# Low halves of streamed weights by an adding DMA in place of a subtraction on VectorE

## The chip, the cores and the metric

The kernel runs on one core of a Trainium2 chip. A core has five engines with queues of their own: TensorE (PE, matmuls), VectorE (DVE), ScalarE (ACT), GpSimd (POOL) and SyncE (SP), which issues most loads. Sixteen DMA engines move the data; transfers are issued from SP's queue or from GpSimd's. The metric is the device time of one execution in microseconds, the median of several runs.

## The reference

A trunk of two layers over 1024 tokens of width 1024, batch 1, fp32, with a vector `c` that modulates both layers:

```python
def even_mixer(h, ...):                       # layer 0
    xa, ga, q, k, v, gb = split(h @ w_in)
    ya = rg_lru(conv4(xa), ...) * silu(ga)
    yb = stick_breaking_attention(rms(q), rms(k), v) * silu(gb)   # 8 heads of 128
    return concat([ya, yb]) @ w_out
def odd_mixer(h, ...):                        # layer 1
    u, g = split(h @ w_in)
    y = gelu(s5_ssm(u, ...))                  # 64 groups of 16 channels, 64 states each
    y = y * sigmoid(y @ glu_w + glu_b)
    return (y * silu(g)) @ w_out
# each layer: x = x + gate * mixer(rms_norm(x) * g * (1 + scale) + shift),
# shift, scale, gate from silu(c) @ ada_w + ada_b
```

## The kernel before

Every fp32 matrix that enters a projection is split into two rounded halves, hi = round(w) and lo = round(w - hi), and a product is the sum of three: hi by hi, hi by lo, lo by hi. Activations lie transposed in SBUF as 8 tiles of 128 x 1024, with a hi and a lo tile each. A weight block is a tile of 128 x 1024 (512 KB) and feeds one projection: 48 matmuls of 512 columns, six for each of 8 k-tiles (lines 120 to 125 of `proj_k`); the fifth of the six is the first that reads the block's low half. In attention, q, k and v of a head come from three blocks of `wqkv` side by side in one pair of tiles, `wqkv_hi` and `wqkv_lo`, and matmuls of 384 columns (lines 771 to 773).

The blocks are streamed. `w_fetch` loads the next of `w_order` one ahead of use: 0 to 7 are the gate weights of the attention heads, 8 to 19 those of the LRU stage, 20 to 35 the output projection of layer 0 (`woe`), 36 to 51 the input projection of layer 1 (`wod`, u and g blocks), 52 to 59 the GLU. There are two hi, two lo and two raw buffers; a hi and a lo buffer come free when the projection before the last has read them. `load_split` issues the load on SP's queue, ScalarE rounds the high half (`w_hi`, line 72), VectorE subtracts (`w_lo`, line 75). `load_qkv` does the same for the three blocks of the next head while the present head still runs. The first three blocks of layer 1 (`w_shifted`) are also read raw by VectorE for the shift's share.

The stages follow one another: norm and head 0; attention head by head, with gates and the next head's q, k, v as filling work, the adaLN columns (`ada_raw`, which share the raw buffers) and the S5 preparation on VectorE; the LRU stage; the output projection, eight blocks against `ya`, eight against `yb`, meanwhile VectorE makes rotation tables which GpSimd stores (`rot_s`); layer 1, where projections alternate with S5 matmuls; eight GLU blocks; the last projection, whose factors GpSimd computes (`st_w`). Only TensorE's order is the order of the code. On the other engines the scheduler of the framework places instructions by its own estimate of when they can run, so an edit moves neighbours as well. Each engine executes its queue in order.

In attention the weights of one query block come from `keep` and `beta`: ScalarE writes both from the scores (lines 820, 823), VectorE scans `keep` (826) and multiplies `beta` by it (827), and TensorE transposes `beta` (837).

Of the kernel before, what the change touches and what calls it, by code (L numbers as in the profile page):

```python
# [9 lines left out]
F32 = mybir.dt.float32  # L10
# [3 lines left out]
AF = mybir.ActivationFunctionType  # L14
ALU = mybir.AluOpType
PSUM = bass.MemoryType.PSUM

P = 128
# [36 lines left out]
class Trunk:  # L55
# [21 lines left out]
    def load_split(self, src, hi, lo):  # L77
# [2 lines left out]
        self.split(raw, hi, lo)  # L80
        return raw

    def w_next(self, ahead=1):

        self.w_fetch(self.w_used + 1 + ahead)
        self.w_used += 1
        return self.w_ready.pop(0)
# [13 lines left out]
    def w_fetch(self, n):  # L101

        while self.w_loaded < min(len(self.w_order), n):
            hi = self.wp.tile([P, 1024], F32R, name="w_hi", tag="whi", bufs=2)
            lo = self.wp.tile([P, 1024], F32R, name="w_lo", tag="wlo", bufs=2)
            raw = self.load_split(self.w_order[self.w_loaded], hi, lo)
            if self.w_loaded in self.w_shifted:
                self.shifted(raw)
            self.w_ready.append((hi, lo))
            self.w_loaded += 1  # L110

# [112 lines left out]
    def run(self):  # L224
        nc, I = self.nc, self.I
        self.cp = self.pool("const")
        self.rp = self.pool("raw", bufs=2)
        self.wp = self.pool("w")
        psp = self.pool("psum", space=PSUM)
        self.bank = [psp.tile([P, 512], F32, name=f"bank{i}") for i in range(8)]  # L230
        self.pair_i = 0
        self.w_order = [I["wfm"][16 + h] for h in range(8)] + [I["wfm"][8]]
        self.lru_order = [(x[:2], int(x[2:])) for x in LRU_ORDER.split()]
        names = {"ga": "ga", "xa": "xa", "ga": "ga", "cv": "conv", "gt": "gates", "dc": "decays"}
        self.lru_order = [(names[kind], m) for kind, m in self.lru_order]
        self.w_order += [I["wfm"][m + (8 if kind == "ga" else 0)] for kind, m in self.lru_order if kind in ("ga", "xa")]
        for half in range(2):
            self.w_order += [I["woe"][m][:, half * 1024:(half + 1) * 1024] for m in range(8)]
        self.s5_order = self.plan_s5()
        self.w_odd, self.w_shifted, self.wsh = len(self.w_order), set(), []  # L240
        self.w_order += [I["wod"][m + (8 if kind == "g" else 0)] for kind, m in self.s5_order if kind in "ug"]
        self.w_order += [I["wglu"][m] for m in range(8)]
        self.w_used = self.w_loaded = 0
        self.w_ready = []
        self.setup()
        self.hp = self.pool("h0")
        self.hh = self.hp.tile([P, KT, T], F32R, name="h_hi")
        self.hl = self.hp.tile([P, KT, T], F32R, name="h_lo")
        self.layer0_norm()
        self.attention()  # L250
        self.lru()
        self.out_even()
        self.layer1()
        psp.release()
# [61 lines left out]

    def load_qkv(self, hd, c):
        cs = slice(c * 1024, (c + 1) * 1024)
        self.load_split(self.I["wqkv"][hd][:, cs], self.wqh[:, cs], self.wql[:, cs])

    def layer0_norm(self):

# [1316 lines left out]
```

## Time and profile before

| | us |
|---|---|
| median of 3 runs | 1342.17 |
| lowest, highest | 1341.04, 1342.34 |
| the profiled execution, its own time | 1343.34 |
| its span | 1341.3 |
| TensorE busy | 1316.6 |
| VectorE busy | 1010.6 |
| ScalarE busy | 651.8 |
| GpSimd busy | 228.9 |

The span is what the hardware profiler saw from the first instruction to the last; 2.0 us lie around it. A group of instructions has a line number of the kernel, the tile written and the tiles read, the busy time and the mean of one, and the idle time in front of it with what ended it. A line can be that of a helper: line 75 is every subtraction of a split, so the tile's name tells which. A wait that several events end is put down to the last of them.

### The profile page before, as it was taken

What the parts mean: (1) busy time and instruction counts of PE and PEld (TensorE: products, weight loads), DVE (VectorE), ACT (ScalarE), POOL (GpSimd) and SP (SyncE); (2) the same over time, 40 slices, a digit from 0 to 9 for tenths busy, and PEclk for the clock granted to TensorE, in tenths of its full rate; (3) what the DMA queues carried; (4) which work ended last, traced back from release to release, by engine and by line L of the source; (5) the groups of instructions that cost most, each with busy time, mean ns of one, the idle gap of its engine ahead of it and who ended that gap; (6) DMA issues with size and microseconds to landing.
All of it is one profiled execution on the core that took longest, in us unless ns stands there. A gap on an engine that the chain in (4) does not pass through costs nothing.

```text
span 1341.3 us, 18939 instructions
## 1 busy us (share of the span) xinstructions
PE 1316.6 (98%) x7020; PEld 1137.7 (85%) x7020; DVE 1010.6 (75%) x1826; ACT 651.8 (49%) x1218; POOL 228.9 (17%) x411
## 2 busy tenths in 40 slices
PE   7998999999999999999999999999999999999998
PEld 3898989898999999988878878888888888888777
DVE  7949977777787868787999787866588669755653
ACT  6545454545454545455998621132463434632421
POOL 1012322222222222210000000000000000000784
PEclk9999999999999999999999999999999999999999
DMA  8443141414141414213112164342458778444331
GB/s 324 166 149 95 58 142 37 146 34 145 34 145 34 147 33 158 85 63 110 36 40 67 61 230 136 115 145 99 135 164 247 229 246 245 122 163 133 108 112 76
DMA packets 73356, 168.22 MB, mean 125 GB/s; under 512 B 9552, under 2 KB 35408, under 8 KB 73264
## 3 DMA queue, kind: packets, MB, share of 16 engines
q1 hardware_dynamic: 62256, 128.40, 31.3%
q0 software_dynamic: 11008, 38.62, 7.8%
q8 instruction: 55, 0.90, 0.3%
q14 instruction: 37, 0.30, 0.1%
HBM read 126.16 MB, written 40.83 MB: 125 GB/s over the span
## 4 chain that ended last, share of the span: by engine, by line
PE 78%; DVE 13%; ACT 3%; issue 3%; DMA 2%; POOL 1%; DVEq 0%; ACTq 0%; POOLq 0%
PE bank L120 6%; PE bank L121 6%; PE bank L123 6%; PE bank L122 6%; PE bank L124 6%; PE bank L125 6%; PE bank L771 6%; PE bank L773 6%; PE bank L772 6%; PE bank L837 2%; PE bank L199 2%; PE bank L197 2%; PE bank L198 2%; DMA ada_raw<-ada 2%; PE bank L849 1%
## 5 line engine op out<-in xcount | busy, mean ns | idle before, releaser
L771 PE MATMUL bank<-wqkv_hi,h_hi 128*128 128x384 f32 x512 | 173.6, 339 | 0.0
L773 PE MATMUL bank<-wqkv_hi,h_lo 128*128 128x384 f32 x512 | 172.3, 337 | 0.0
L772 PE MATMUL bank<-wqkv_lo,h_hi 128*128 128x384 f32 x512 | 172.3, 337 | 0.0
L72 ACT CAST w_hi<-w_raw 128x1024 fp32r<-128x1024 f32 x60 | 63.0, 1050 | 193.5 <-PE bank L123 148.5
L75 DVE TENSOR_TENSOR w_lo<-w_raw,w_hi 128x1024 fp32r<-128x1024 f32 x60 | 73.0, 1218 | 41.2 <-ACT w_hi L72 41.1
L771 PEld LDWEIGHTS bank<-wqkv_hi,h_hi 128*128 128x128 f32 x512 | 96.6, 189 | 0.3
L772 PEld LDWEIGHTS bank<-wqkv_lo,h_hi 128*128 128x128 f32 x512 | 96.6, 189 | 0.4
L773 PEld LDWEIGHTS bank<-wqkv_hi,h_lo 128*128 128x128 f32 x512 | 96.5, 189 | 0.0
L120 PE MATMUL bank<-h_hi,w_hi 128*128 128x512 f32 x224 | 89.1, 398 | 0.0
L122 PE MATMUL bank<-h_hi,w_hi 128*128 128x512 f32 x224 | 87.6, 391 | 0.8 <-DVE xc L1014 0.8
L124 PE MATMUL bank<-h_hi,w_lo 128*128 128x512 f32 x224 | 87.7, 392 | 0.4 <-DVE w_lo L75 0.4
L121 PE MATMUL bank<-h_lo,w_hi 128*128 128x512 f32 x224 | 87.7, 391 | 0.0
L123 PE MATMUL bank<-h_lo,w_hi 128*128 128x512 f32 x224 | 87.5, 390 | 0.0
L125 PE MATMUL bank<-h_hi,w_lo 128*128 128x512 f32 x224 | 87.4, 390 | 0.0
L778 ACT ACTIVATE nat<-bank 128x128 f32<-128x128 f32 x64 | 17.7, 277 | 141.3 <-PE bank L773 137.9
L826 DVE TENSOR_TENSOR_SCAN keep<-keep,diag 128x1024 f32<-128x1024 f32 (+3 forms) x64 | 86.2, 1347 | 0.1
L314 POOL TENSOR_SCALAR ss<-ss 128x2 f32<-128x2 f32 x64 | 28.6, 446 | 296.6 <-ACT nat L779 296.1
L820 ACT ACTIVATE keep<-bank,ss 128x512 f32<-128x512 f32 (+2 forms) x96 | 54.5, 597 | 21.7 <-PE bank L819 20.1
L783 DVE SCALAR_TENSOR_TENSOR nat<-bank,ss,gqk 128x128 f32<-128x128 f32 x64 | 22.1, 345 | 47.9 <-PE bank L837 25.9
L823 ACT ACTIVATE beta<-bank,ss 128x512 f32<-128x512 f32 (+3 forms) x96 | 54.4, 600 | 0.0
L290 DVE SCALAR_TENSOR_TENSOR ada_raw<-ada_raw,cs 128x1024 f32<-128x1024 f32 x39 | 47.6, 1220 | 7.8 <-DMA ada_raw<-ada 7.5
L315 POOL TENSOR_TENSOR ss<-ss,mh 128x2 f32<-128x2 f32 x64 | 51.9, 810 | 5.3
(436 smaller groups left out, 3739.2 us busy)
## 6 DMA issues: line engine op xcount, KB each, us to landing
ada_raw<-ada SPq DMA_DIRECT2D x39, 512.0 KB, 3.9
w_raw<-wqkv SPq DMA_DIRECT2D x21, 512.0 KB, 3.6
w_raw<-wfm SPq DMA_DIRECT2D x20, 512.0 KB, 3.6
w_raw<-woe SPq DMA_DIRECT2D x16, 512.0 KB, 3.8
w_raw<-wod SPq DMA_DIRECT2D x16, 512.0 KB, 4.4
x<-xT SPq DMA_DIRECT2D x8, 512.0 KB, 7.1
cx_s<-ce POOLq DMA_DIRECT2D x16, 256.0 KB, 2.7
win_s<-wsb POOLq DMA_DIRECT2D x16, 256.0 KB, 3.5
```

Of the source, the lines that this page charges most:

```text
L72: nc.scalar.copy(hi, raw)
L75: nc.vector.tensor_sub(lo, raw, hi.bitcast(F32))
L120: nc.tensor.matmul(ps[0], wh[:, k, :], rh[k][:, h0], start=first, stop=False)
L121: nc.tensor.matmul(ps[0], wh[:, k, :], rl[k][:, h0], start=False, stop=False)
L122: nc.tensor.matmul(ps[1], wh[:, k, :], rh[k][:, h1], start=first, stop=False)
L123: nc.tensor.matmul(ps[1], wh[:, k, :], rl[k][:, h1], start=False, stop=False)
L124: nc.tensor.matmul(ps[0], wl[:, k, :], rh[k][:, h0], start=False, stop=last)
L125: nc.tensor.matmul(ps[1], wl[:, k, :], rh[k][:, h1], start=False, stop=last)
L771: nc.tensor.matmul(ps[:, 0:384], hh[:, k, ts], wqh[:, ks], start=(k == 0), stop=False)
L772: nc.tensor.matmul(ps[:, 0:384], hh[:, k, ts], wql[:, ks], start=False, stop=False)
L773: nc.tensor.matmul(ps[:, 0:384], hl[:, k, ts], wqh[:, ks], start=False, stop=(k == KT - 1))
L826: v.tensor_tensor_scan(rev, rev, self.diag[:, T - n:T][:, ::-1], 0.0, op0=ALU.mult, op1=ALU.max)
```

## The change

A new `load_split_dma` takes the place of `load_split` for 68 blocks: the blocks 0 to 9 and 20 to 59 of `w_order` except the three shifted ones (47), and the 21 of `load_qkv`. It loads the raw tile as before and lets ScalarE round the high half; then ScalarE writes the negated high half into the low tile, -round(w) from the raw tile, and a DMA issued by GpSimd adds the block once more from DRAM onto that tile, which leaves w - hi. The subtraction on VectorE is gone for these blocks. The ten LRU blocks 10 to 19, the shifted ones, head 0's first q, k, v blocks and all splits of activations stay.

```diff
--- before.py
+++ after.py
@@ -80,6 +80,15 @@
         self.split(raw, hi, lo)
         return raw
 
+    def load_split_dma(self, src, hi, lo):
+
+        nc = self.nc
+        raw = self.rp.tile([P, 1024], F32, name="w_raw", tag="raw")
+        nc.sync.dma_start(raw, src)
+        nc.scalar.copy(hi, raw)
+        nc.scalar.activation(lo, raw, AF.Copy, scale=-1.0)
+        nc.gpsimd.dma_start(lo, src, accum_op=ALU.add)
+
     def w_next(self, ahead=1):
 
         self.w_fetch(self.w_used + 1 + ahead)
@@ -103,9 +112,12 @@
         while self.w_loaded < min(len(self.w_order), n):
             hi = self.wp.tile([P, 1024], F32R, name="w_hi", tag="whi", bufs=2)
             lo = self.wp.tile([P, 1024], F32R, name="w_lo", tag="wlo", bufs=2)
-            raw = self.load_split(self.w_order[self.w_loaded], hi, lo)
-            if self.w_loaded in self.w_shifted:
-                self.shifted(raw)
+            if self.w_loaded in self.w_plain:
+                self.load_split(self.w_order[self.w_loaded], hi, lo)
+            elif self.w_loaded in self.w_shifted:
+                self.shifted(self.load_split(self.w_order[self.w_loaded], hi, lo))
+            else:
+                self.load_split_dma(self.w_order[self.w_loaded], hi, lo)
             self.w_ready.append((hi, lo))
             self.w_loaded += 1
 
@@ -234,6 +246,7 @@
         names = {"ga": "ga", "xa": "xa", "ga": "ga", "cv": "conv", "gt": "gates", "dc": "decays"}
         self.lru_order = [(names[kind], m) for kind, m in self.lru_order]
         self.w_order += [I["wfm"][m + (8 if kind == "ga" else 0)] for kind, m in self.lru_order if kind in ("ga", "xa")]
+        self.w_plain = range(10, len(self.w_order))
         for half in range(2):
             self.w_order += [I["woe"][m][:, half * 1024:(half + 1) * 1024] for m in range(8)]
         self.s5_order = self.plan_s5()
@@ -316,7 +329,7 @@
 
     def load_qkv(self, hd, c):
         cs = slice(c * 1024, (c + 1) * 1024)
-        self.load_split(self.I["wqkv"][hd][:, cs], self.wqh[:, cs], self.wql[:, cs])
+        self.load_split_dma(self.I["wqkv"][hd][:, cs], self.wqh[:, cs], self.wql[:, cs])
 
     def layer0_norm(self):
```

The lines of the changed kernel stand 13 further down from `w_fetch` on. Three places show what else moves.

VectorE, head 0 of attention. Between the scan (`keep<-keep,diag`) and the product `beta<-beta,keep` of the first query block there stood before one adaLN pass (`ada_raw`) and six products of the S5 preparation (`t`, `bb`):

```order
L826 SCALAR_TENSOR_TENSOR keep<-keep,diag 128x1024
L633 TENSOR_TENSOR s5small<-s5small 128x32
L290 SCALAR_TENSOR_TENSOR ada_raw,mod<-ada_raw,cs 128x1024
L641 TENSOR_TENSOR t_1104<-bb,s5small 128x512
L642 TENSOR_TENSOR t_1105<-bb,s5small 128x512
L643 TENSOR_TENSOR bb<-bb,s5small 128x512
L645 TENSOR_TENSOR bb<-bb,s5small 128x512
L644 TENSOR_TENSOR bb<-bb,t_1105 128x512
L646 TENSOR_TENSOR bb<-bb,t_1104 128x512
L1130 TENSOR_SCALAR lsmall<-cols 128x8
L827 TENSOR_TENSOR beta<-beta,keep 128x1023
```

and now, from the last three of those products on:

```order
L657 TENSOR_TENSOR bb<-bb,t_1107 128x512
L658 TENSOR_TENSOR bb<-bb,s5small 128x512
L701 TENSOR_TENSOR ce<-craw,pw 128x2x144
L659 TENSOR_TENSOR bb<-bb,t_1106 128x512
L1143 TENSOR_SCALAR lsmall<-cols 128x8
L839 SCALAR_TENSOR_TENSOR keep<-keep,diag 128x1024
L1144 TENSOR_TENSOR lsmall<-lsmall,cols 128x8
L690 COPY bd<-bb 64x8x16
L222 TENSOR_SCALAR lsmall<-lsmall 128x8
L840 TENSOR_TENSOR beta<-beta,keep 128x1023
```

The products stand ahead of the scan and the adaLN pass has gone elsewhere; three small operations are left between scan and product.

GpSimd, from attention into the output stage, before (`yb_s` is the last head's result on its way to DRAM, `rot_s` the rotation tables):

```order
L727 DMA win_s_1119<-wsb 128x512
L734 DMA rp_s_1135<-rpad 128x240
L967 DMA yb_s_616<-yb 128x1024
L1220 DMA rot_s_7771<-rot 128x1024
L1220 DMA rot_s_7772<-rot 128x1024
L1220 DMA rot_s_7773<-rot 128x1024
```

and now:

```order
L740 DMA win_s_1121<-wsb 128x512
L747 DMA rp_s_1137<-rpad 128x240
L980 DMA yb_s_618<-yb 128x1024
L90 DMA w_lo<-woe 128x1024 x2
L1233 DMA rot_s_7811<-rot 128x1024
L90 DMA w_lo<-woe 128x1024 x2
L1233 DMA rot_s_7812<-rot 128x1024
```

The low halves of two blocks go ahead of the first `rot_s`, the third waits behind it.

ScalarE, first half of layer 1 (`x<-x,mod,gain` is the modulation of the normed activations, `h_hi` their split, `ub` and `ut` the early u blocks), before:

```order
L1253 COPY ub<-bank_75 128x1
L1260 ACTIVATE x_7271<-x_7271,mod,gain 128x1024
L1298 ACTIVATE ut<-ut,ub 128x512 x2
L72 CAST w_hi<-w_raw 128x1024
L1260 ACTIVATE x_7271<-x_7271,mod,gain 128x1024 x4
L72 CAST h_hi<-x_7271 128x1024 x3
L1253 COPY ub<-bank_76 128x1
L72 CAST h_hi<-x_7271 128x1024 x2
```

and now:

```order
L1266 COPY ub<-bank_75 128x1
L1273 ACTIVATE x_7303<-x_7303,mod,gain 128x1024
L1311 ACTIVATE ut<-ut,ub 128x512 x2
L88 CAST w_hi<-w_raw 128x1024
L1273 ACTIVATE x_7303<-x_7303,mod,gain 128x1024 x4
L89 ACTIVATE w_lo<-w_raw 128x1024
L72 CAST h_hi<-x_7303 128x1024 x2
L1266 COPY ub<-bank_76 128x1
L72 CAST h_hi<-x_7303 128x1024 x2
```

The pass that writes the negated half (`w_lo`) stands behind four modulations and ahead of the splits.

## Rows read from the trace of the kernel before

**Rows 1.** Page: busy time by engine; a group: busy us, mean ns, idle before

```profile
PE 1316.6 (98%) x7020; PEld 1137.7 (85%) x7020; DVE 1010.6 (75%) x1826; ACT 651.8 (49%) x1218; POOL 228.9 (17%) x411
...
L72 ACT CAST w_hi<-w_raw 128x1024 fp32r<-128x1024 f32 x60 | 63.0, 1050 | 193.5 <-PE bank L123 148.5
```

**Rows 2.** VectorE by line, splits of streamed weights: busy us, mean ns

```profile
L75 DVE TENSOR_TENSOR w_lo<-w_raw,w_hi 128x1024 fp32r<-128x1024 f32 x60 | 73.0, 1218 | 41.2 <-ACT w_hi L72 41.1
...
L75 DVE TENSOR_TENSOR wqkv_lo<-w_raw,wqkv_hi 128x1024 fp32r<-128x1024 f32 x21 | 25.7, 1222 | 7.0 <-ACT wqkv_hi L72 7.0
```

**Rows 3.** Waits of TensorE, whole span: us in total, times, longest

```profile
PE bank L837 <- DVE beta L827: 3.1, 4, 2.1
...
PE bank L121 <- DVE rot L1205: 0.6, 1, 0.6
```

**Rows 4.** Timeline of TensorE in head 0: start, duration, idle before, releaser

```profile
114.03 0.66 PE L798 MATMUL bank<-ident,nat 128*128 128x128 f32 x4 [1.59 <-DVE nat L783]
...
131.74 1.09 PE L837 MATMUL bank<-ident,beta 128*128 128x128 f32 x8 [2.07 <-DVE beta L827]
```

**Rows 5.** Windows in head 0: us, busy by engine, clock, DMA share, GB/s

```profile
113.00:114.00 1.00, 0.00 (x0) 0.00 (x0) 1.00 (x3) 0.00 (x0) 0.75 (x1) 1.00 0.65 90
132.00:137.00 5.00, 5.00 (x24) 5.00 (x23) 4.55 (x11) 3.47 (x8) 2.87 (x4) 0.66 0.00 0
```

**Rows 6.** Timeline of VectorE in head 0

```profile
112.50 1.21 DVE L75 TENSOR_TENSOR wqkv_lo<-w_raw,wqkv_hi 128x1024 fp32r<-128x1024 f32 x1
113.64 0.34 DVE L783 SCALAR_TENSOR_TENSOR nat<-bank,ss,gqk 128x128 f32<-128x128 f32 x1
...
123.35 2.28 DVE L826 TENSOR_TENSOR_SCAN keep<-keep,diag 128x1024 f32<-128x1024 f32 x1
...
130.46 1.22 DVE L827 TENSOR_TENSOR beta<-beta,keep 128x1023 f32<-128x1023 f32 x1
```

**Rows 7.** Timeline of ScalarE in head 0

```profile
122.67 0.70 ACT L823 ACTIVATE beta<-bank,ss 128x511 f32<-128x511 f32 x1
```

**Rows 8.** DMA issues: queue, count, KB each, median us to landing

```profile
w_raw<-woe SPq DMA_DIRECT2D x16, 512.0 KB, 3.8
...
rot_s<-rot POOLq DMA_DIRECT2D x8, 512.0 KB, 2.9
...
us<-ut POOLq DMA_DIRECT2D x8, 512.0 KB, 7.2
...
gs_s<-sg POOLq DMA_DIRECT2D x8, 512.0 KB, 5.1
...
ada_w<-adak SPq DMA_DIRECT2D x2, 512.0 KB, 9.0
```

**Rows 9.** Timeline of GpSimd: output stage and end of layer 1

```profile
788.15 0.54 POOL L1220 DMA_DIRECT2D rot_s<-rot  x1 [163.00 <-DVE rot L1219]
...
1164.34 0.53 POOL L1311 DMA_DIRECT2D gs_s<-sg  x1 [12.39 <-DVE sg L537]
```

**Rows 10.** Window in the output stage, columns as in rows 5

```profile
775.00:780.00 5.00, 4.43 (x19) 3.30 (x19) 3.74 (x13) 2.00 (x2) 0.00 (x0) 1.00 1.02 419
```

**Rows 11.** Timeline of ScalarE: output stage and start of layer 1

```profile
762.27 1.05 ACT L72 CAST w_hi<-w_raw 128x1024 fp32r<-128x1024 f32 x1
...
783.40 1.06 ACT L72 CAST w_hi<-w_raw 128x1024 fp32r<-128x1024 f32 x1 [5.69 <-DMA w_raw<-woe]
...
973.11 4.64 ACT L1260 ACTIVATE x<-x,mod,gain 128x1024 f32<-128x1024 f32 x4
```

**Rows 12.** Timeline of TensorE: first read of a low half in four projections

```profile
768.41 0.39 PE L124 MATMUL bank<-ya,w_lo 128*128 128x512 f32 x1
...
791.23 0.39 PE L124 MATMUL bank<-ya,w_lo 128*128 128x512 f32 x1
...
981.52 0.39 PE L124 MATMUL bank<-h_hi,w_lo 128*128 128x512 f32 x1
...
1170.87 0.39 PE L124 MATMUL bank<-y_hi,w_lo 128*128 128x512 f32 x1
```

## The prediction

> **What bounds the kernel now.** I read the busy times first: TensorE works 98% of the span, VectorE 75%, ScalarE 49%, GpSimd 17% [rows 1]. So what the change takes from VectorE counts only where TensorE stands still, and I read TensorE's waits next. VectorE's share of them that the change can touch is small: four waits for `beta` (3.1 us, of which one is 2.07), one for `nat` (1.59), one of 0.6 (near 778) that the list puts on a memset, behind a low half of `ya` that VectorE had just split [rows 3, 4]. The other idle time lies at the start, inside the LRU stage, in the last phase where GpSimd subtracts, or on loads, and is left as it is. The clock comes third: after the 2.07 us the granted clock averages 0.66 over 132 to 137 us, with part of it at the lower level (1.2 of 2.4 GHz); while TensorE stood still for 1.59 us at 113 the row shows 1.00 [rows 4, 5]. The first stall therefore cost 2.07 + 5 x 0.34 = 3.8 us.
>
> **What goes and comes.** 68 loads change (47 of `w_fetch`, 21 of `load_qkv`). VectorE loses 47 x 1.218 + 21 x 1.222 = 82.9 us [rows 2]; ScalarE gains a second pass of the size of its first, 68 x 1.05 = 71 us [rows 1], which brings it to 54%; GpSimd gains 68 issues of about 0.54 us [rows 9], 37 us; the DMA engines move 68 x 0.524 = 35.7 MB more. None of these totals is a time: the terms are four places.
>
> **Gain, attention.** The order of VectorE in head 0 shows where 2.07 us go. Before, one pass over adaLN weights and six 512-wide products stand between the scan and `beta`; now the products come ahead of the scan, in the time of three removed subtractions (3.66 us), and the pass elsewhere. ScalarE has the scan's second half ready at 122.67 + 0.70 = 123.4 in either kernel; then the scan's 2.28 us and two or three small operations, so `beta` starts near 125.9 instead of 130.46 and TensorE asks at 129.67 [rows 4, 6, 7]. The stall goes, and the half-clock stretch with it: 3.8 us. The other three `beta` waits, 3.1 - 2.07 = 1.0, follow head boundaries where three subtractions leave VectorE; I take all of it. The `nat` wait: a subtraction ran from 112.50 until `nat` started at 113.64 [rows 6]. Two are gone from its front, but small operations of the S5 preparation have moved in there, and ScalarE's second pass delays the sums of squares by up to 1.05. Between 0 and 1.59 I take 0.4. The 0.6 near 778 goes, since two subtractions ahead of that split are gone. Gain: 3.8 + 1.0 + 0.4 + 0.6 = 5.8 us.
>
> GpSimd's queue now also holds the adding transfers ahead of norm operations at each head boundary, and they wait there for ScalarE's pass. I cost that at nothing: `nat` is waited for once in the whole trace, and TensorE has scores and gates of the old head to do meanwhile; without that cover it would be a pass of 1.05 us in each of seven heads.
>
> **The new chain.** Elsewhere a weight's low half was ready 1.2 us after its high half. Now it is high half, ScalarE's negative pass (1.05), GpSimd's issue, landing. Call L the time from issue to landing. The trace of before has no adding transfer. Below it is bounded by GpSimd's quickest 512 KB, 2.9 us, above by the slowest 512 KB load of the list, 9.0 [rows 8]. The same bytes of the output weights land in 3.8 by the plain queue; a second operand to be read makes it longer by up to 0.52 MB at the rate of the DMA engines when full, 419 GB/s, 1.25 us [rows 8, 10]. I take L = 5.0, nearest the 3.8 row.
>
> The Trainium skill (DMA: Bandwidth & Descriptors, "Anatomy of one DMA — SWDGE (gpsimd) path") fits a transfer issued by GpSimd as 2.0 us + bytes / 436e3, 3.2 us for 512 KB. It also says (Collectives: The Full Stack, "The bandwidth ceiling") that a DMA's add reads both operands, which would make the estimate 4.4; GpSimd's own rows of 2.9 to 7.2 us in this trace [rows 8] do not follow such a fit. By 4.4 the sum below would come out at -2.8, the edge of the faster case.
>
> **Where L is paid.** Both weight buffers are free only when the projection before the last is done, so there is one projection for all of it: the first low halves of the first and third output blocks are read 22.8 us apart, 0.6 of it waiting [rows 3, 12], 11.1 us for one. Four places have less.
> First projection of the output stage: ScalarE is behind with the end of the LRU, starts the high half at 762.27, negates until 764.4; the first low half is read at 768.41 [rows 11, 12]: TensorE waits L - 4.0.
> Third one: its raw tile lands late behind eight loads of `x`; high half at 783.40, negated by 785.5; but in GpSimd's queue the store of `rot_s` stands ahead, which started at 788.15 and comes at most 1.2 earlier (one subtraction less on VectorE), plus 0.54 to issue: 787.5 to 788.7. Read at 791.23 [rows 9, 11, 12]: L - 3.7 to L - 2.5, I take L - 3.1. It contains the first wait, since a delayed TensorE also asks later; it is not added to it. The second weight's transfer runs beside those loads at full DMA engines [rows 10] and has 7 us, so it is covered unless L passes 7.
> Fourth projection of layer 1, the first one after the three shifted weights: four modulations of 1.16 us are queued on ScalarE between the high half and the negative pass, until 977.7; negated at 978.8, read at 981.52 [rows 11, 12]: L - 2.7. Before, VectorE did this subtraction meanwhile and nothing waited.
> First GLU projection: its transfer stands on GpSimd behind the store of `gs_s`, which starts at 1164.34 and takes 0.53; the low half is read at 1170.87 [rows 9, 12]: L - 6.0.
> Everything else has more room: in attention and where S5 work lies between the projections an L of 9 is covered; the other output and GLU projections pay from L of about 9 on (11.1 us less two passes and an issue).
> The 35.7 MB may slow the loads that S5 work waits for, by a microsecond or two; I leave that out of the sum and in the range.
>
> **The sum.** At L = 5: third output projection 1.9, fourth of layer 1 2.3, nothing at the GLU. The clock: 1.59 us of idle time kept it, 2.07 did not [rows 4, 5], so the 2.3 gets 1.7 on top, the 1.9 none. Losses 5.9, gain 5.8: +0.1 on the profiled 1343.34 us (span 1341.3). That run lies 1.2 above the median of the three (1342.17), which the next kernel's will be compared with: 1343.44 - 1.17, forecast **1342.3 us**.
> For other L: 4.0 gives 0.9 + 1.3 - 5.8 = -3.6 (1338.6); 4.4, 1.3 + 1.7 - 5.8 = -2.8; 6.0, 2.9 + 3.3 + 3.4 (two clock losses) - 5.8 = +3.8 (1346.0); 7.0, 3.9 + 4.3 + 3.4 + 1.0 - 5.8 = +6.8 (1349.0); 9.0, 5.9 + 6.3 + 3.4 + 3.0 - 5.8 = +12.8 (1355.0), before any steady projection pays.
>
> **Rivals.**
> Faster: the adding transfer lands like GpSimd's quick stores (2.9 to 4.4) and only the attention gain is left: 1336.6 to 1339.4. For it speak the rows of 2.9 and an idle queue [rows 8, 9], against it the second operand.
> Slower: it lands in 5.3 to 7 us. Mechanism and place are the same two first reads of a low half; it decides from L = 5.3 on, because then both stalls pass 2.07 us and both cost the clock too: 1345 to 1349. For it speak GpSimd's stores of 5.1 and 7.2 us and the full DMA engines around 778 [rows 8, 10].
> Much slower: the addition itself is slow, 7 to 9 us or more. From 9 on each of some twenty back-to-back projections waits: 1349 to 1357 and beyond. No row speaks for it or against it.
> It changes nothing: VectorE's stalls only move to what is late next (ScalarE, with its 71 us more, in front of the same `beta`), and the transfers stay hidden: within 2 us of today. Against it: ScalarE idles half the time.
>
> **How the numbers follow.** Landing in 4.4 to 5.3 (gain and loss cancel) 0.35; faster 0.26; slower 0.23; much slower 0.13; nothing changes 0.03. 0.2% is 2.7 us, about what can be told apart here. Faster by more 0.26, within 0.38, slower 0.36. The range of 1337.5 to 1354 leaves out the lowest fifth of the faster case (0.05) and most of the much slower one (0.1).
>
> **What would show it.** The attention step holds if the wait for `beta` at about 130 us and the 0.66 after it are gone; it fails if TensorE still waits there for VectorE, or for ScalarE. The list of DMA issues will give L as `w_lo` from GpSimd; TensorE's waits must then name that transfer in the output stage near 790 and in layer 1 near 981, with L - 3.1 and L - 2.7. Waits in every projection from 800 on mean the much slower case. If L is 5 and neither place waits, the chain of release and queues is wrong, not the price; if `nat` waits at head boundaries, the cover that I gave GpSimd's queue was not there.

## The result: 6.5% slower, more than half of it in attention

The changed kernel takes 1429.31 us (median of 4 runs, 1426.79 to 1432.22) against 1341.61 us for the kernel before (4 runs beside it, 1341.03 to 1342.34). The ratio is 1.0654, 95% interval 1.0631 to 1.0677: slower by 88 us, far outside the range that was given (1337.5 to 1354).

The page of the kernel after, in the columns of [rows 1] (first line), then its queues (packets, MB, share of 16 engines' span):

```profile
PE 1340.0 (94%) x7020; PEld 1154.2 (81%) x7020; DVE 937.5 (66%) x1758; ACT 715.7 (50%) x1286; POOL 281.4 (20%) x479
...
q1 hardware_dynamic: 62256, 128.40, 29.6%
q0 software_dynamic: 20800, 74.27, 20.5%
```

The work moved as the diff says: VectorE lost 73 us against [rows 1], ScalarE gained 64, GpSimd 53. But TensorE, with the same 7020 matmuls, is busy 23.4 us longer, most of it by the clock (an estimate of 20 us, from windows of 0.25 us: eleven stretches at a lowered clock, where the kernel before has one), and idle for 1428.7 - 1340.0 = 88.7 us instead of 24.7. 23.4 + 64.0 is the whole difference of the spans, 87.4 us.

The list of DMA issues of the kernel after, columns as in [rows 8], then one row and the second queue of the kernel before:

```profile
ada_raw<-ada SPq DMA_DIRECT2D x39, 512.0 KB, 6.0
w_raw<-wqkv SPq DMA_DIRECT2D x21, 512.0 KB, 4.0
wqkv_lo<-wqkv POOLq DMA_DIRECT2D x21, 512.0 KB, 8.6
...
w_lo<-woe POOLq DMA_DIRECT2D x16, 512.0 KB, 7.8
...
w_lo<-wod POOLq DMA_DIRECT2D x13, 512.0 KB, 8.2
```
```profile
q0 software_dynamic: 11008, 38.62, 7.8%
...
ada_raw<-ada SPq DMA_DIRECT2D x39, 512.0 KB, 3.9
```

The adding transfer, L in the prediction, lands in 7.8 to 8.6 us (medians of its groups), not in 5.0. And a load that the diff doesn't touch became slower: `ada_raw`, 6.0 us where the same row of before has 3.9.

TensorE's waits in the kernel after, columns as in [rows 3]:

```profile
PE bank L850 <- DVE beta L840: 35.9, 6, 6.8
PE bank L136 <- DMA w_lo<-woe: 9.7, 4, 3.6
PE bank L1393 <- DMA tz<-rp_s: 8.0, 4, 2.7
...
PE bank L136 <- DMA w_lo<-wod: 4.7, 1, 4.7
PE bank L136 <- DMA w_lo<-wglu: 4.3, 3, 2.6
```

The first line is the surprise: the product whose wait was to vanish, 3.1 us before, is now waited for 35.9 us, at six head boundaries (in heads 1 to 6, where the first is head 0). It waits for VectorE, the engine that the change relieved.

Where the time came in, by the moment at which TensorE reaches the same instruction (timelines of four kernels, us; e1 and e2 are the halves of the change, below):

```
                                         before   after    e1       e2
first low half, output stage             768.41   821.57   818.52   770.09
first product, layer 1                   943.32  1007.56   993.47   950.97
first product of S5 input, layer 1       991.70  1062.96  1041.85  1007.06
first high half, GLU                    1169.94  1250.73  1219.11  1192.81
first low half, last phase              1257.48  1343.44  1306.67  1285.89
```

After minus before: 53.2 us up to the output stage (3.6 of them its first wait), 11.1 in the output stage, 16.5 in layer 1 (7.0 of them in its first four projections, before the S5 input), 5.2 in the GLU stage, 1.4 behind it.

### One head boundary

VectorE at the boundary of heads 0 and 1 (the expectations below call it that of heads 1 and 2), kernel before (start, duration, instruction, idle before): the adaLN passes (L290), the scan (L826), `beta` (L827).

```profile
187.89 1.22 DVE L290 SCALAR_TENSOR_TENSOR ada_raw<-ada_raw,cs 128x1024 f32<-128x1024 f32 x1
...
193.90 1.23 DVE L290 SCALAR_TENSOR_TENSOR ada_raw<-ada_raw,cs 128x1024 f32<-128x1024 f32 x1 [0.67 <-DMA ada_raw<-ada]
...
195.05 2.29 DVE L826 TENSOR_TENSOR_SCAN keep<-keep,diag 128x1024 f32<-128x1024 f32 x1
...
198.45 1.22 DVE L827 TENSOR_TENSOR beta<-beta,keep 128x1023 f32<-128x1023 f32 x1
```

The same place in the kernel after, VectorE and then TensorE's matmul that reads `beta`:

```profile
192.00 1.22 DVE L303 SCALAR_TENSOR_TENSOR ada_raw<-ada_raw,cs 128x1024 f32<-128x1024 f32 x1 [0.98 <-issue]
...
198.26 1.23 DVE L303 SCALAR_TENSOR_TENSOR ada_raw<-ada_raw,cs 128x1024 f32<-128x1024 f32 x1 [4.59 <-DMA ada_raw<-ada]
...
201.50 1.23 DVE L303 SCALAR_TENSOR_TENSOR ada_raw<-ada_raw,cs 128x1024 f32<-128x1024 f32 x1 [1.34 <-DMA ada_raw<-ada]
...
203.14 1.22 DVE L303 SCALAR_TENSOR_TENSOR ada_raw<-ada_raw,cs 128x1024 f32<-128x1024 f32 x1 [0.21 <-DMA ada_raw<-ada]
...
204.29 2.28 DVE L839 TENSOR_TENSOR_SCAN keep<-keep,diag 128x1024 f32<-128x1024 f32 x1
...
207.08 1.21 DVE L840 TENSOR_TENSOR beta<-beta,keep 128x1023 f32<-128x1023 f32 x1
```
```profile
208.44 1.94 PE L850 MATMUL bank<-ident,beta 128*128 128x128 f32 x8 [5.63 <-DVE beta L840]
```

ScalarE has the second half of the scan's operand ready early in the kernel after:

```profile
195.17 0.69 ACT L833 ACTIVATE keep<-bank,ss 128x512 f32<-128x512 f32 x1
```

So the scan could have started at 195.9. It starts at 204.3, because four passes over adaLN weights stand ahead of it in VectorE's queue, whose order is fixed when the program is built (before, three of the four), and these passes wait for their loads: 4.59 + 1.34 + 0.21 us of idle VectorE. The loads are late for two reasons, both in the issue rows of SyncE (start, duration, instruction), before and after:

```profile
180.55 11.75 SPq L280 DMA_DIRECT2D ada_raw<-ada  x4
```
```profile
186.52 13.33 SPq L293 DMA_DIRECT2D ada_raw<-ada  x4
```

The first starts 6.0 us later: these loads take the two raw buffers over from the weight blocks, and block 1's buffer is now free only after ScalarE's second pass, which stands behind other work at 185.44 (before, VectorE's subtraction was through at 180.5). And they take longer: the four of this boundary land in 3.6 to 8.8 us, median 6.8, where before they took 4.3 to 5.5, median 4.5. They run beside the adding transfers, while the DMA engines are full, as the first of these windows of the kernel after shows (stretch, busy us of PE, PEld, DVE, ACT, POOL, granted clock, DMA share, GB/s).

```profile
186.00:199.00 13.00, 13.00 (x61) 10.85 (x61) 6.65 (x15) 7.56 (x12) 3.67 (x5) 1.00 1.04 297
199.00:207.00 8.00, 3.81 (x22) 3.49 (x21) 6.41 (x11) 1.88 (x4) 0.00 (x0) 0.87 0.72 201
207.00:211.00 4.00, 2.56 (x11) 2.59 (x12) 3.95 (x5) 3.43 (x9) 1.82 (x4) 0.50 0.60 180
```

Its last line is the second charge: after 5.63 us of standing still TensorE has the lower of its two levels, 1.2 GHz, for the whole stretch. The same picture repeats at 282, 356, 429, 504 and 578 us, with waits of 5.6 to 6.8.

### The profile page after: what moved, and what is told of

It is laid out like the page before. It is cut to its first block, busy times and chain, and to the rows that moved or that the text cites. A ratio compares the mean times of both kernels' runs of the same rounds, so it can differ in the third digit from the quotient of the medians.

```text
span 1428.7 us, 19057 instructions
## 1 busy us (share of the span) xinstructions
PE 1340.0 (94%) x7020; PEld 1154.2 (81%) x7020; DVE 937.5 (66%) x1758; ACT 715.7 (50%) x1286; POOL 281.4 (20%) x479
## 3 DMA queue, kind: packets, MB, share of 16 engines
q0 software_dynamic: 20800, 74.27, 20.5%
## 4 chain that ended last, share of the span: by engine, by line
PE 55%; DMA 15%; DVE 12%; issue 11%; ACT 5%; POOL 2%; SPq 1%; POOLq 0%; DVEq 0%; ACTq 0%
DMA ada_raw<-ada 5%; PE bank L784 5%; PE bank L785 5%; PE bank L786 5%; PE bank L136 3%; PE bank L137 3%; PE bank L132 3%; PE bank L133 3%; PE bank L135 3%; PE bank L134 3%; DMA cx<-cx_s 3%; PE bank L850 2%; DMA w_raw<-wqkv 2%; DVE keep L839 2%; DMA w_lo<-wglu 2%
## 5 line engine op out<-in xcount | busy, mean ns | idle before, releaser
L88 ACT CAST w_hi<-w_raw 128x1024 fp32r<-128x1024 f32 x47 | 49.3, 1050 | 210.2 <-PE bank L135 125.6
L850 PE MATMUL bank<-ident,beta 128*128 128x128 f32 x288 | 47.2, 301 | 38.9 <-DVE beta L840 35.9
L850 PEld LDWEIGHTS bank<-ident,beta 128*128 128x128 f32 x288 | 36.2, 155 | 42.5 <-ACT nat L792 13.9
L1354 DVE TENSOR_TENSOR m<-L,rot 128x1024 f32<-128x1024 f32 x32 | 37.7, 1220 | 43.4 <-DMA rot<-rot_s 29.7
L327 POOL TENSOR_SCALAR ss<-ss 128x2 f32<-128x2 f32 x64 | 20.9, 327 | 199.4 <-ACT nat L792 198.3
L853 DVE TENSOR_TENSOR wt_lo<-bank,wt_hi 128x512 fp32r<-128x512 f32 (+1 forms) x96 | 50.4, 547 | 12.4 <-ACT wt_hi L852 12.4
```

The lines of the kernel that those rows point to most:

```text
L850: nc.tensor.transpose(tr[:, kb - b0, :], beta[:, kb * P:(kb + 1) * P], self.ident)
```

## The experiments

Where no number of runs is given, a time is that of one run, beside one run of the kernel before. The 25 runs of the kernel before that stand beside e8 lie between 1340.18 and 1344.46 us, so a difference of a few us between single runs shows nothing.

### The two halves of the change

**e1** keeps the adding transfer for the query, key and value blocks only (`load_qkv`); **e2** for the blocks of `w_fetch` only.

```diff
 e1, in w_fetch
-                self.load_split_dma(self.w_order[self.w_loaded], hi, lo)
+                self.load_split(self.w_order[self.w_loaded], hi, lo)
 e2, in load_qkv
-        self.load_split_dma(self.I["wqkv"][hd][:, cs], self.wqh[:, cs], self.wql[:, cs])
+        self.load_split(self.I["wqkv"][hd][:, cs], self.wqh[:, cs], self.wql[:, cs])
```

> Only the 21 blocks of load_qkv get the adding transfer; all blocks of w_fetch are split as before. Theory: attention lost its 49 us through these blocks alone (their raw buffers and their transfers hold back the adaLN loads, and the four adaLN passes stand ahead of the first scan on VectorE), so 1385 to 1395 us, TensorE waits for beta near 6 us at six head boundaries, and no wait for w_lo of a DMA. Rival: the loss in attention comes from the extra traffic of all 68 transfers, gate blocks included; then under 1375.

> Only the 47 blocks of w_fetch get the adding transfer; q, k, v blocks are split as before. Theory: what is left is the waits for w_lo in the output stage, at the fourth projection of layer 1 and in the GLU, waits for S5 loads and the half-clock stretches behind them, 38 us in the changed kernel: 1374 to 1384 us, and the waits for beta at head boundaries stay under 1 us. Rival (all transfers together): over 1395.

Measured: e1 1392.21 us, +48.9 on the kernel before beside it (1343.33); waits for `beta` 35.9 us at six places, no wait for a low half that a DMA writes. e2 1372.4, +29.1; waits for `w_lo<-woe` 8.3, `w_lo<-wod` 4.9, `w_lo<-wglu` 2.6, `tz` 7.7 us, `beta` 2.7. So 49 us belong to 21 transfers at the head boundaries, and the 47 others cost 29 us. The two sum to 78 of 88. By the table above, some 5 of the missing 10 us lie in the output stage (11.1 us lost with both halves, 6.0 in e2, none in e1) and some 2 in layer 1 (16.5 against 15.2 in e2 and a gain of 1.0 in e1); why the halves cost more together there is not shown. Another 2 may lie in attention: e2's first low half of the output stage is at 770.09 although it is waited for 4.06 us, so its attention was about 2 us faster than before's. (e12, below, does not bear these 2 us out: its interval reaches from 2.1 us faster to 0.9 slower.)

### The place of the adaLN passes

**e6** leaves all 68 adding transfers and queues each head's four adaLN passes on VectorE behind the first `beta` product.

```diff
+            if i == 7:
+                first_product[:] = [product]
...
-                self.ada_cols(*ada[4 * hd + j])
+                with self.tc.issue_after(first_product[0].ins):
+                    self.ada_cols(*ada[4 * hd + j])
```

> The changed kernel with one order changed: the four adaLN passes of each head are queued on VectorE behind the first product for beta instead of ahead of the first scan; loads and transfers stay. Theory (the 49 us of attention are passes that wait for late loads, in front of the scan in VectorE's queue): the beta waits at head boundaries fall from 36 us in all to under 6, the half-clock stretches behind them go, time 1378 to 1390. Rival (attention waits for something else of the new chain, such as a low half of q, k, v that lands late): another wait takes their place and the time stays above 1410.

Measured: 1383.94 us, 45.4 less than the changed kernel. The waits for `beta` are gone. VectorE at the same boundary in e6:

```profile
195.42 2.29 DVE L841 TENSOR_TENSOR_SCAN keep<-keep,diag 128x1024 f32<-128x1024 f32 x1 [3.83 <-ACT keep L835]
197.81 1.23 DVE L842 TENSOR_TENSOR beta<-beta,keep 128x1023 f32<-128x1023 f32 x1
...
199.56 1.22 DVE L303 SCALAR_TENSOR_TENSOR ada_raw<-ada_raw,cs 128x1024 f32<-128x1024 f32 x1
```

The scan now waits 3.83 us for ScalarE, its real input, and `beta` is 9.3 us earlier than in the kernel after. The adding transfers are no faster here (`wqkv_lo` lands in 9.8 us), and attention doesn't care. The output stage begins at 774.82, of which 3.8 are its first wait: against 768.41 about 2.6 of the 49 us are left. This shows the cause in attention: the loss is made by passes that wait for late loads in front of the scan (e5, below, shows heads without such passes).

**e8** puts the same order into the kernel before, which has no adding transfer.

> The kernel before, without any adding transfer, with one edit of order: in every head the four passes over the adaLN weights of the next head are queued on VectorE behind the first beta product. Theory (an adaLN pass queued ahead of the scan is what makes TensorE wait for beta): the wait of 2.07 us near 130 falls by about one pass of 1.2, to 1 us or less, and no longer pulls the clock down, so 1.2 + 1.7 go, and the two smaller beta waits of 0.4 and 0.3 go with it: 1338 to 1339.5, against 1341.6 for the kernel before. Rival (the passes only take the place of something else: what they feed comes late, or nat waits behind them): the sum of waits of VectorE stays at 5 us or more and the time stays within 1341 to 1345.

Measured: 1346.12 us (10 runs) against 1341.84 (25), ratio 1.0029, interval 1.0020 to 1.0039: slower by 0.3%. The stall near 130 us is gone as expected (the stretch 128 to 138 us, 7.93 us busy before, is full at clock 1.00), but the passes now delay the next products: waits for `wt_lo` at L853 are 4.5 us in 8 places. My expectation was wrong, for the theory and for the rival's range of 1341 to 1345; the passes have to be somewhere, and the order of the kernel before is the better one for fast loads.

### Why the adaLN loads are late

**e4** makes the negated half from the high half, so that the raw buffer is free after ScalarE's first pass. **e3** makes the second transfer a plain copy: the traffic stays, the addition goes. **e9** adds from the raw tile in SBUF instead of from DRAM, which holds the raw buffer until the transfer has landed.

```diff
 e4
-        nc.scalar.activation(lo, raw, AF.Copy, scale=-1.0)
+        nc.scalar.activation(lo, hi.bitcast(F32), AF.Copy, scale=-1.0)
 e3
-        nc.gpsimd.dma_start(lo, src, accum_op=ALU.add)
+        nc.gpsimd.dma_start(lo, src)
 e9
-        nc.gpsimd.dma_start(lo, src, accum_op=ALU.add)
+        nc.gpsimd.dma_start(lo, raw, accum_op=ALU.add)
```

> The negated half is made from the high half instead of the raw tile, so that the raw buffer comes free after the first ScalarE pass. Theory A (the late release of the raw buffers delays the adaLN loads): at the boundary of heads 1 and 2 the first adaLN load starts about 3.6 us earlier, the beta waits fall from 5.6-6.8 to under 3.5 us, time 1400 to 1412. Theory B (the adding transfers hold the DMA engines while the adaLN loads run, which took 8.8 and 8.2 us there): the beta waits fall by less than 1.5 us, time above 1418.

> The GpSimd transfers stay, in number, place and bytes from DRAM, but copy the block over the low half instead of adding it; the low half is then the block itself, so this kernel computes something else. Theory: the addition makes the transfer slow (issue to landing 8 us, and more of the DMA engines' time for each byte): without it 4 to 5 us, waits for w_lo gone or under 1 us, beta waits at head boundaries under 3 us, 1340 to 1365 us in all. Rival: the time goes into GpSimd's queue and the extra bytes; then landing stays above 6.5 us and the time above 1400.

> The adding transfer reads the raw tile in SBUF instead of the block in DRAM, which keeps the raw buffer until it has landed; nothing else changes. It prices the second source: if the read from DRAM makes the transfer slow, the gate blocks' landing (7.9 us) falls under 6; if the addition itself does, it stays between 7 and 9. The raw buffers are held some 8 us longer, so by the theory of late buffers the time goes up, to 1445 to 1500 us.

Measured: e4 1406.7 us (waits for `beta` 25.7), e3 1393.98 (17.2), e9 1404.43 (13.6). In e4 the loads start at 182.65 instead of 186.52, 3.9 us earlier, and 23 of the 88 us go, though the loads of `ada_raw` land in 7.4 us, later than in the kernel after (6.0), and each wait for `beta` stays above 4 us: the late buffer is one cause, not the only one. In e3 35 us go, where I had expected 64 or more: without the addition the loads are still late, and the fixed order still hands that on. Its second queue and its rows of DMA issues give the price of the addition:

```profile
q0 software_dynamic: 20800, 74.27, 15.2%
...
wqkv_lo<-wqkv POOLq DMA_DIRECT2D x21, 512.0 KB, 6.4
...
w_lo<-wfm POOLq DMA_DIRECT2D x10, 512.0 KB, 4.5
```

Against 8.6 and 7.9 us in the kernel after, the addition adds 2.2 and 3.4 us to a landing; for `woe`, `wod` and `wglu` it adds 2.0, 0.9 and 2.3. In e9 the order of the loads is another, and it was faster where I expected it slower by 15 to 70 us:

```profile
w_lo<-w_raw POOLq DMA_DIRECT2D x47, 512.0 KB, 5.3
ada_raw<-ada SPq DMA_DIRECT2D x39, 512.0 KB, 3.6
```

So an addition whose second operand lies in SBUF lands in 5.3 us (5.5 for the 21 of `wqkv`), and the adaLN loads are as fast as before. Its attention is still slow; what stands against it is that the raw buffers are held longer (adaLN loads at the boundary from 193.51). The three edits overlap: their gains (23, 35, 25 us) are not terms of one sum, since each shortens the same chain of load, pass, scan.

**e5** gave the adaLN loads two buffers of their own.

```diff
-                self.ada_cols(*ada[4 * hd + j])
+                raw = early.tile([P, D], F32, name="ada_own", tag="ada_own", bufs=2)
+                self.ada_load(*ada[4 * hd + j], raw=raw)
+                self.ada_cols(*ada[4 * hd + j], raw=raw)
```

> The changed kernel with two buffers for the adaLN loads in attention alone, so that they share none with the raw tiles of the streamed blocks. Theory A (shared buffers that the second ScalarE pass frees late hold the loads back): the first two passes find their data, the beta waits fall under 2 us each, 1375 to 1395 us. Theory B (the adding transfers slow the loads themselves): the loads still land in 7 to 9 us beside them and the beta waits stay above 3.5 us, over 1405 us.

Measured: 1403.92 us, between the two ranges. As a test of A against B it is inconclusive, for it changed two things at once: with free buffers the scheduler drew passes of later heads into the first ones, where `nat` is now waited for 7.3 us in 4 places. But all 32 loads are issued by 240 us, so the later heads have the adding transfers and no adaLN pass. The window from 300 to 600 us, columns as above:

```profile
300.00:600.00 300.00, 299.78 (x1903) 284.09 (x1902) 187.73 (x360) 169.07 (x448) 78.75 (x193) 1.00 0.32 83
```

Twelve adding transfers of `load_qkv` fall into it, which land in 9.1 us, and TensorE stands still for 0.2 us (1.9 in the same window of the kernel before). The adding transfers by themselves cost these heads nothing; with e6 this leaves the adaLN passes and their late loads.

### Does attention gain anything?

**e7** uses the adding transfer for the three blocks that are loaded during head 0 alone: the place of the forecast's largest gain, without the later boundaries.

```diff
+        load = self.load_split_dma if hd == 1 else self.load_split
+        load(self.I["wqkv"][hd][:, cs], self.wqh[:, cs], self.wql[:, cs])
```

> Only the three q, k, v blocks that are loaded during head 0 get the adding transfer; all else is split as before. The prediction's gain in head 0, by itself: the wait of 2.07 us for beta at 130 us and the clock loss behind it go, 1339 to 1341 us beside 1342 to 1343. Rival: what the trace of the changed kernel shows between 138 and 160 us (six small waits of 4 us for ScalarE and wt_lo) eats it: 1342 to 1346.

Measured: 1341.55 us against 1341.72, no difference that single runs can show. The windows behind [rows 5], first of the kernel before, then of e7:

```profile
128.00:138.00 10.00, 7.93 (x40) 7.61 (x39) 9.55 (x22) 5.00 (x12) 2.87 (x4) 0.83 0.14 49
138.00:165.00 27.00, 27.00 (x187) 26.39 (x186) 26.73 (x79) 13.50 (x42) 9.84 (x19) 1.00 0.24 72
```
```profile
128.00:138.00 10.00, 9.36 (x58) 8.77 (x57) 9.94 (x32) 4.94 (x17) 3.53 (x7) 1.00 0.05 15
138.00:165.00 27.00, 25.22 (x168) 23.74 (x169) 25.46 (x65) 13.16 (x39) 8.03 (x17) 1.00 0.32 106
```

The stall and the lowered clock are gone (7.93 to 9.36 us busy, 0.83 to 1.00). The next 27 us, full before, have holes of 1.78 us: small waits for `wt_lo` (VectorE) and for `beta` and `wsb` (ScalarE, up to 0.70 each). The two traces show the same in times: TensorE begins the first `beta` product of head 0 at 130.42 instead of 131.74, 1.3 us earlier, and that of head 1 at 199.97 instead of 199.72. What one product gained, the next ones gave back. That S5 preparation and ScalarE's work moved behind it is the likely reason; no run separates it.

**e12** uses the adding transfer only for the blocks 0 to 9 of `w_order` (the eight gate blocks of the heads and the first two of the LRU stage), **e13** adds e6's order to that. In both, `load_qkv` and all blocks from 10 on are split by VectorE.

```diff
-            if self.w_loaded in self.w_plain:
+            if self.w_loaded >= 10 and self.w_loaded not in self.w_shifted:
```

> Only the ten gate blocks of layer 0 (the head's gate weights in attention) are made by the adding transfer; the query, key and value blocks, the output, layer-1 and GLU blocks are split by VectorE as before. Theory (attention loses by the three adding transfers of each head boundary, which share a raw buffer with the adaLN loads; the gate blocks have their own time and lose nothing): the attention gain of about 2.4 us that the kernel with all of w_fetch adding showed remains, and no loss behind it: 1338.5 to 1340. Rival (every adding transfer in attention delays the loads beside it): no gain, 1341.5 to 1346, with waits for beta of 1 us or more at several boundaries.

> The ten gate blocks made by the adding transfer, all else split by VectorE, and the four adaLN passes of each head queued on VectorE behind the first beta product. Theory: both gains are in attention but at different places (the passes at the head boundary, the subtraction of the gate block in the middle of a head), so they add for the most part: 1336.5 to 1339. Rival (both shorten the same stalls, or the passes crowd what the lighter VectorE had room for): no better than the better one of the two alone, 1339 to 1342.

Measured: e12 1341.14 us (10 runs), ratio 0.9995 (0.9984 to 1.0007); e13 1342.05 (10 runs), 0.9998 (0.9988 to 1.0008). Neither is faster. No version of this change that was run beats the kernel before, and the best ones are those with least of it.

### Layer 1 alone

**e14** uses the adding transfer for the layer-1 blocks from the fifth on and nowhere else: twelve of the thirteen, not nine from the fourth on as its expectation says. The fourth block (39 in `w_order`), whose low half TensorE waits 4.69 us for in the kernel after, is split by VectorE here.

```diff
-            if self.w_loaded in self.w_plain:
+            if self.w_loaded not in range(40, 52) and self.w_loaded not in self.w_shifted:
```

> Only nine of the layer-1 projection blocks (from the fourth on) are made by the adding transfer; all else is split by VectorE as before. Theory (the loss of layer 1 is made in layer 1: the first unshifted projection waits for its low half, and the S5 loads tz and yt wait beside the adding transfers): a wait for w_lo of about 4.9 us near 985, waits for tz of 5 to 8 us in three or four places, and about 1.7 us of clock behind each wait over 2 us: 1350 to 1358. Rival (layer 1 loses because the output stage in front of it hands over late and in another order): only the 4.9 us with its clock, 1345 to 1348.5.

Measured: 1356.06 us, +14.2. TensorE's waits for DMA in e14:

```profile
PE bank L1393 <- DMA tz<-rp_s: 7.6, 4, 2.6
...
PE bank L136 <- DMA w_lo<-wod: 2.0, 1, 2.0
```

Layer 1 makes its loss by itself: 14 us here without the fourth block, 16.5 in the kernel after with it. Most of the 14 is not a low half: the S5 tiles `tz`, which SyncE loads, land beside the adding transfers in 4.6 us (3.6 before) and are waited for 7.6 us, where the kernel before does not wait for them. The stretch 1060 to 1100 us has the DMA engines at 0.98 of their time for 266 GB/s. The 2.0 us are the fifth projection's.

## Why the prediction was wrong, step by step

**TensorE is the bound, totals are not times.** Right. VectorE lost 73 us of work and the kernel lost 88 us of time. The totals themselves came out at 73, 64 and 53 us for VectorE, ScalarE and GpSimd, where the prediction had 83, 71 and 37; the issue of an adding transfer takes GpSimd 0.85 to 0.94 us, not 0.54. None of them is a term of the sum.

**Gain in attention, 5.8 us.** Wrong: no run shows a gain. The stall near 130 us and its clock went, but e7's traces show the time given back by the next head: I followed one product past VectorE and did not look at the ones behind it. Even the stall did not go as worked out. In the kernel after an adaLN pass and six products stand ahead of the scan, which starts at 127.42, so `beta` starts at 129.88, not at 125.9. TensorE finds it ready because it comes 1.8 us later itself, at 131.48; that part was luck. ([rows 7] is also not the scan's operand but the second half of `beta`; that of `keep` is written just before it.) Of the other terms only the 0.6 near 778 appears: its row is gone from the list of waits. The three small `beta` waits became the 35.9 us, and `nat` is waited for 1.7 us by VectorE and 1.5 by ScalarE where it was 1.59 [rows 4].

**"In attention ... an L of 9 is covered", and GpSimd's queue at nothing.** This is the step that failed, though each sentence is true as far as it goes. TensorE never waits for a `wqkv_lo`, and `nat` waits at no later head boundary. What I left out is what shares something with the new transfers: the raw buffers, which ScalarE's second pass holds and the adaLN loads need next, and the DMA engines, in which those loads run beside them. Both delays reach TensorE through a fixed order on VectorE. The test that the prediction named could not show this. e1 gives 49 us for it, e6 takes 45 of the 88 away by moving the passes alone, and in e5 the heads without these passes lose nothing.

**L, taken as 5.0 with bounds of 2.9 and 9.0.** Mis-sized: 7.8 to 8.6 by the list, inside the bounds and near the upper one. I had taken the load of the same bytes on the other queue, 3.8, and up to 1.25 for the second operand. Both were too small: GpSimd's plain copies in these places take 4.5 to 7.3 (e3), and in four of five groups the addition adds 2.0 us or more. The fit of the Trainium skill (DMA: Bandwidth & Descriptors, "Anatomy of one DMA — SWDGE (gpsimd) path") gives an estimate of 3.2 us for 512 KB; the trace of e3, with its 4.5 to 7.3, does not agree. The added 35.65 MB kept the 16 engines 20.5% of 1428.7 less 7.8% of 1341.3 us, 188 us or 2.77 us a transfer, and without the addition (e3, 15.2% of 1392.2) 107 us or 1.57. The Trainium skill says of the add in a collective's reduce step that it needs two source reads (Collectives: The Full Stack, "The bandwidth ceiling"); the 1.8 times longer share here agrees.

**The four places.** Right in place and mechanism. The first reads of a low half there, kernel after:

```profile
821.57 0.50 PE L136 MATMUL bank<-ya,w_lo 128*128 128x512 f32 x1 [3.58 <-DMA w_lo<-woe]
...
846.97 0.50 PE L136 MATMUL bank<-ya,w_lo 128*128 128x512 f32 x1 [1.54 <-DMA w_lo<-woe]
```
```profile
1050.83 0.80 PE L136 MATMUL bank<-h_hi,w_lo 128*128 128x512 f32 x1 [4.69 <-DMA w_lo<-wod]
```
```profile
1254.44 0.50 PE L136 MATMUL bank<-y_hi,w_lo 128*128 128x512 f32 x1 [2.62 <-DMA w_lo<-wglu]
```

L - 4.0 = 3.58 gives L = 7.6; L - 3.1 = 3.58 + 1.54 gives 8.2 (the third contains the first, as said); L - 2.7 = 4.69 gives 7.4; L - 6.0 = 2.62 gives 8.6, of which 1.2 are the issue coming later than assumed (GpSimd waits 0.76 us for ScalarE's pass there). At L = 8 the prediction's own rules give 1352: the mis-sized L explains 10 us of the miss, the rest is elsewhere.

**"The other projections pay from L of about 9 on."** Wrong, for the queue, not for L. Waits of 1.86 and 2.73 us stand at 893 and 941 in the output stage too. GpSimd's timeline ahead of the second:

```profile
934.45 0.55 POOL L1197 DMA_DIRECT2D x_s<-x  x1 [7.70 <-DVE rot L1232]
935.04 0.88 POOL L90 DMA_DIRECT2D w_lo<-woe  x1
```

ScalarE had negated this weight at 928.6; the transfer stood 6.5 us behind a store that waited for VectorE. I had walked GpSimd's queue at the third projection and at the GLU only.

**"35.7 MB may slow the loads that S5 work waits for, by a microsecond or two".** Mis-sized: `tz` is waited for 8.0 us, and e14 puts 14 us on layer 1 alone, without the fourth projection's wait.

**Clock, 1.7 us for a stall over 2.07.** About right on average: TensorE's busy time grew by 23.4 us with 14 such stalls besides the old one for `diag`, less the one that went, 1.8 each. Stall by stall the rule fails. The first row follows the wait of 1.86 us at 893, the second one of 2.73 at 941, the third another of 2.73 at 1189:

```profile
893.00:899.00 6.00, 5.94 (x19) 4.71 (x20) 5.48 (x14) 0.00 (x0) 1.23 (x2) 0.72 0.63 192
941.00:947.00 6.00, 5.55 (x17) 4.43 (x18) 2.42 (x2) 1.78 (x2) 1.34 (x2) 0.72 1.00 308
1189.00:1195.00 6.00, 5.74 (x42) 5.38 (x43) 1.42 (x2) 3.16 (x4) 0.57 (x2) 1.00 1.02 313
```

Four stalls of 2.4 to 2.7 us (at 1097, 1189, 1254 and 1366) left the clock at 1.00; those of 1.86 and of 2.73 at 941 were followed by a lower one. So the length of a stall did not decide alone, and that the price came out right on average is luck. The stalls of 5.6 to 6.8 us all lowered the clock: 200 to 300 us has a mean of 0.93 with two of them.

**Still open.** Whether a late buffer or a slow load is the larger cause in attention: e3, e4 and e9 each shorten the same chain and shift the order a little. The GLU and output stage were not run by themselves, nor the fourth projection of layer 1. And what besides its length makes a stall lower the clock was not tested.

## What to carry to other kernels

When an operation moves to another engine, list what the moved work shares besides time: the buffer it now holds longer, the queue it stands in, the transfers it runs beside. Then look for the instruction of a fixed order that waits for any of these, and for what is queued behind it; an engine with a third of its time free stalls TensorE when a load-bound pass stands in front of its one urgent operation. And a stall that is taken away is a gain only when the products behind it have been followed too.

## What the runs showed of the hardware

In the kernel after, an adding DMA from DRAM onto 512 KB in SBUF lands in 7.8 to 8.6 us (medians of its groups). With the operand in SBUF it lands in 5.3 to 5.5 (e9), as a plain copy by the same queue in 4.5 to 7.3 (e3). By the queue's share of time it keeps the 16 DMA engines 2.77 us, the plain copy 1.57. Beside the adding transfers the 512 KB adaLN loads by the other queue went from 3.9 to 6.0 us. Taking VectorE's subtractions away in head 0 (e7) removed a stall of 2.07 us with its lowered clock, and one head later TensorE was where it had been, within 0.3 us. Of two stalls of TensorE of 2.73 us each, one was followed by a granted clock of 0.72 over 6 us, the other by 1.00; one of 1.86 us was followed by 0.72.
